# Products 5 and 7 in another order, and weights' lower parts by an adding DMA, in a two-block transformer layer kernel

## The chip, the cores and the metric

The kernel runs on one core of a Trainium2 chip. The metric is the device time of one execution, in microseconds. Engines are named as in the profile: PE (TensorE's matmuls) and PEld (its weight loads), DVE (VectorE), ACT (ScalarE), POOL (GpSimd) and SP (SyncE, which issues most DMAs here).

## What is computed

Two transformer blocks run one after the other on 512 tokens of width 1024; the first block puts 16 meta tokens in front (528 columns). Each block is a SwiGLU feed-forward layer, a token mixer, and another SwiGLU layer, with norms between them. All is in float32.

```python
def first_block(x, ...):                       # 16 + 512 tokens
    h = h + 0.5 * rmsnorm(swiglu(rmsnorm(h, gn[0]), ffn_w_in[0], ffn_w_out[0]), gn[1])
    y = mlstm_mixer(rmsnorm(h, gn[2]), a_w_in, a_conv_w, a_conv_b, a_gate_b, a_w_out)
    h = h + rmsnorm(y, gn[3])
    h = h + 0.5 * rmsnorm(swiglu(rmsnorm(h, gn[4]), ffn_w_in[1], ffn_w_out[1]), gn[5])
    return h[:, 16:]

def second_block(x, ...):                      # 512 tokens
    h = h + 0.5 * swiglu_2(rms_norm(h, ...), w_gate, w_up, w_down)
    proj = rms_norm(h, ...) @ w_in             # latent attention (8 heads) and retention (8 heads)
    h = h + concat([mla_group(...), retention_group(...)]) @ w_o
    h = h + 0.5 * swiglu_2(rms_norm(h, ...), w_gate, w_up, w_down)
    return rms_norm(h, final_norm)

def swiglu(x, w_in, w_out):                    # d_ff = 2816
    gu = x @ w_in
    return (silu(gu[..., :D_FF]) * gu[..., D_FF:]) @ w_out
```

## The kernel before, in words

**Split products.** Activations stand in SBUF with features on the partitions. Every large product is made of three matmuls in the round format fp32r: weights' higher part times activations' higher part, higher times lower, lower times higher. A weight tile of 128x1024 (a "unit") arrives by DMA in one of two raw tiles (`raw0`, `raw1`, and `rawx` beside them in the feed-forward layers). `Weights.pump` (from line 107) then splits it into a slot: ACT writes the rounded higher part `whi` (line 120), and `lo_engine` subtracts that from the raw tile and writes the lower part `wlo` (line 121). There are four to six slots; a unit is split as soon as a slot comes free, so some units stand ready ahead of PE. When the last unit of a raw tile is split, SP loads the next but one raw tile into it (`self.dma(r + 3)`).

`lo_engine` is DVE in the feed-forward layers and POOL in the two mixers: line 1129, from the fifth product of the first mixer (mLSTM), and line 1339, for the second mixer (latent attention and retention).

**Sevens.** In the feed-forward layers the last 16 of 22 chunks of 128 hidden features are computed by Strassen-Winograd products (`Ffn.seven`, from line 699; its matmuls are issued by `product`, line 696): seven products of 12 matmuls each in place of eight, over two halves of the tokens (264 or 256 columns). One chunk has P1 to P7. P1 and P2 use the unit "gates", P5 and P7 the unit "twos" (its first and second half), P6, P4 and P3 half units. P1, P6, P7 and P4 add up in one PSUM bank (`sa`, `o.a` in the code), with a copy to SBUF by ACT after P1, P6 and P7 (`m1`, `m2`, `m3`); P5 and P3 add up in another (`sc`, `o.c`), P2 has a third (`sb`). After P7 and P5, DVE makes `c22 = o.c + m3`. P4 and P3 of a chunk are written in the program inside the next chunk (`up_a(old)`, `gate_b(old)`). There are 8 runs of 8 chunks in the kernel: two in each of the four feed-forward layers.

A chunk's "gates" unit is split late: `W.hold` keeps it back until the copy `m3` of the chunk before, and `tc.issue_after(last.ins)` puts the cast behind that copy on ACT's queue.

**Order of the work.** The program is written as one sequence, and a scheduling layer then orders the instructions of each engine by its own estimate of when things are ready. So what stands in the source order (P5, P7, P1, P2, P4, P6, P3) is interleaved on PE's queue: parts of P4, P3, P1 and P2 stand mixed. Every engine works through its queue in order.

**Mixers.** In both mixers PE's queue alternates between the input projections (units of 24 matmuls, twice that over two column ranges in the first block) and attention steps. DVE and ACT evacuate, convolve, mask and normalize; POOL has some casts and subtractions of queries and keys (lines 1080, 1081, 1539), the masks (`affine_select`, line 1158), the lower parts of the weights (line 121) and a few DMAs.

Of the kernel before, what the change touches and what calls it, by code (L numbers as in the profile page):

```python
# [8 lines left out]
F32 = mybir.dt.float32  # L9
# [54 lines left out]
class Weights:  # L64
# [42 lines left out]
    def pump(self):  # L107
        nc = self.nc
        while self.n_split < len(self.subs):
            r, make, half = self.subs[self.n_split]  # L110
            if self.hold and self.raws[r][2] and self.raws[r][1] == 5:
                break
            idle = self.idle_halves if half else self.idle
            if not idle:
                break
            slot = idle.pop(0)
            self.dma(r + 1)
            unit, splits = make(self.raw_tiles[r], slot.hi, slot.lo)
            for ho, lw, src in splits:
                nc.scalar.copy(out=ho, in_=src)  # L120
                self.lo_engine.tensor_tensor(out=lw, in0=src, in1=ho.bitcast(F32), op=ALU.subtract)  # L121
            unit.slot = slot
            self.units.append(unit)
            self.n_split += 1
            self.raws[r][1] -= 1
            if self.raws[r][1] == 0:
                del self.raw_tiles[r]
            if self.raws[r][1] == 0:
                self.dma(r + 3)
            if self.raws[r][2] and self.raws[r][1] == 2 and self.n_raw == r + 2 and self.raws[r + 2][2]:  # L130
                self.load(r + 2, True)
# [88 lines left out]
def two_blocks(ctx: ExitStack, tc, d, out):  # L220
# [407 lines left out]
    class Ffn:  # L628
# [70 lines left out]
        def seven(self, fs, below):  # L699
# [25 lines left out]
            for f in fs:  # L725
                o = Unit(None, None)
                o.f = f
                (u,) = W.take(1)
                o.a, b = ps("sa")[:, 0:n], ps("sb")[:, 0:n]
                self.product(o.a, u, 0, "P1", True)  # L730
                m1 = yt("ht", n)
                act.copy(out=m1, in_=o.a)
                self.product(b, u, 1, "P2", True)
                o.s1, t = self.tmp("a", n), self.tmp("b", n)
                dve.tensor_tensor(out=o.s1, in0=b, in1=m1, op=ALU.add)
                act.activation(out=t, in_=o.s1, func=ACTF.Tanh, scale=0.5)
                W.release(u)
                if old:
                    up_a(old)
                dve.scalar_tensor_tensor(out=o.s1, in0=t, scalar=1.0, in1=o.s1, op0=ALU.add, op1=ALU.mult)  # L740
                (u,) = W.take(1)
                self.product(o.a, u, 0, "P6")
                o.m2 = yt("rp", n)
                act.copy(out=o.m2, in_=o.a)
                W.release(u)
                if old:
                    gate_b(old)
                (u,) = W.take(1)
                o.c = ps("sc")[:, 0:n]
                self.product(o.c, u, 0, "P5", True)  # L750
                self.product(o.a, u, 1, "P7")
                m3 = yt("sqFalse", n)
                last = act.copy(out=m3, in_=o.a)  # L753
                o.c22 = yt("sqacc", n)
                dve.tensor_tensor(out=o.c22, in0=o.c, in1=m3, op=ALU.add)
                W.hold = False
                with tc.issue_after(last.ins):
                    W.release(u)
                W.hold = True
                o.u2, o.u4 = W.take(2)  # L760
                old = o
# [364 lines left out]
    make = {"k": lambda n: item_qk("k", n), "q": lambda n: item_qk("q", n), "v": item_v, "o": item_o}  # L1126
    lead = [Item(1, ev_gate, done_gate)] + [make[k](n) for k, n in order[:3]]
    run_lead(lead, br)
    W.lo_engine = pool
    for k, n in order[3:6]:  # L1130
        run_item(make[k](n), AB)
    cm_s, sp = open_pool("mixs")
# [203 lines left out]
    close_pool(cm_w2)  # L1336


    W.lo_engine = pool
    cm_b, bp = open_pool("mixb")  # L1340
    hsp = drp.tile([P, KD, SEQ], F32, name="hsp")
    pool.dma_start(out=hsp, in_=h[:, :, NM:TT])
# [489 lines left out]
```

## Time and profile before

| | |
|---|---|
| median of 3 runs | 2091.21 us (2089.55 to 2098.18) |
| the profiled execution's own time | 2091.01 us |
| its span in the profile | 2089.1 us |
| PE busy | 2006.3 us, 96% of the span |
| PEld busy | 1840.6 us, 88% |
| DVE busy | 1549.0 us, 74% |
| ACT busy | 1027.4 us, 49% |
| POOL busy | 326.9 us, 16% |
| mean granted TensorE clock | 0.99 |

The time of a run lies 1.9 us above its span. PE's matmuls overlap: the next one starts before the last has drained, so start-to-start distances tell more than durations, and a stretch in which PE counts as busy may still run at the lower granted clock. The feed-forward layers fill about 0 to 400, 640 to 1400 and 1665 to 2060 us; the first mixer lies at about 400 to 640 us and the second at 1405 to 1665 us.

### The profile page before, as it was taken

To read this page: it belongs to the slowest core of one execution; us is meant where nothing else is said; L and a number is where in the kernel's file an instruction comes from. 1 tells how busy PE (TensorE), PEld (TensorE's weight loads), DVE (VectorE), ACT (ScalarE), POOL (GpSimd) and SP (SyncE) were. 2 spreads that over 40 slices of the span, in tenths; PEclk is the share of its full clock that TensorE was granted. 3 is DMA by queue.
4 is the path that set the end of the run, shared out by engine and by line. 5 is a ranking of instruction groups with operands and counts; after the bars stand their busy time and mean duration, and the time that the engine had idled before them with its cause. 6 is when DMAs were issued, how large, how long until landed. Compare 5 with 4: busy or idle time off the path is not lost.

```text
span 2089.1 us, 34858 instructions
## 1 busy us (share of the span) xinstructions
PE 2006.3 (96%) x13583; PEld 1840.6 (88%) x13583; DVE 1549.0 (74%) x2949; ACT 1027.4 (49%) x1973; POOL 326.9 (16%) x290
## 2 busy tenths in 40 slices
PE   8999999989999999999999999998999999999998
PEld 8999999988889989989998988987777778898998
DVE  6848477787886767758777775877888877676684
ACT  5445255445555445436443543654666643353462
POOL 0011020034430002011000201103222100010200
PEclk9999999999999999999999999999999999999999
DMA  6357565222223327567532766733112153475661
GB/s 186 96 111 152 147 140 135 72 77 81 87 81 110 79 79 156 145 137 146 162 80 77 154 152 137 148 118 104 47 47 61 41 141 100 107 158 133 147 151 55
DMA packets 387851, 237.01 MB, mean 113 GB/s; under 512 B 10427, under 2 KB 383926, under 8 KB 387686
## 3 DMA queue, kind: packets, MB, share of 16 engines
q1 hardware_dynamic: 317446, 192.94, 31.4%
q0 software_dynamic: 69680, 40.62, 14.1%
q8 instruction: 106, 1.74, 0.3%
q10 hardware_dynamic: 560, 1.24, 0.2%
q14 instruction: 59, 0.48, 0.1%
HBM read 230.53 MB, written 4.23 MB: 112 GB/s over the span
## 4 chain that ended last, share of the span: by engine, by line
PE 77%; DVE 12%; ACT 5%; issue 3%; POOL 1%; DMA 1%; ACTq 0%; POOLq 0%; DVEq 0%
PE dn L484 23%; PE sa L696 17%; PE acc L484 11%; PE sc L696 8%; PE sb L696 4%; PE accB L484 3%; PE accA L484 3%; PE wo L484 2%; DVE wlo L121 1%; DVE accF L1206 1%; ACT sqFalse L753 1%; PE p L419 1%; PE ro L1604 1%; ACT whi L120 1%; DVE cv L1067 1%
## 5 line engine op out<-in xcount | busy, mean ns | idle before, releaser
L120 ACT CAST whi<-raw 128x1024 fp32r<-128x1024 f32 (+3 forms) x500 | 392.8, 801 | 360.0 <-PE dn L484 163.2
L121 DVE TENSOR_TENSOR wlo<-raw,whi 128x512 fp32r<-128x512 f32 (+2 forms) x456 | 402.3, 905 | 112.9 <-ACT whi L120 110.4
L484 PE MATMUL dn<-gh,whi 128*128 128x256 f32 (+2 forms) x908 | 277.6, 326 | 0.5 <-ACT gh L465 0.5
L484 PE MATMUL dn<-gl,whi 128*128 128x256 f32 (+2 forms) x908 | 277.7, 326 | 0.0
L484 PE MATMUL dn<-gh,wlo 128*128 128x256 f32 (+2 forms) x908 | 276.9, 325 | 0.0
L484 PE MATMUL acc<-nh,whi 128*128 128x512 f32 (+2 forms) x600 | 196.4, 361 | 8.9 <-DVE y L1212 3.9
L484 PE MATMUL acc<-nl,whi 128*128 128x512 f32 (+2 forms) x600 | 192.0, 355 | 0.0
L484 PE MATMUL acc<-nh,wlo 128*128 128x512 f32 (+2 forms) x600 | 191.6, 354 | 0.0
L484 PEld LDWEIGHTS dn<-gh,whi 128*128 128x128 f32 x908 | 163.0, 188 | 16.5 <-ACT gh L465 0.7
L484 PEld LDWEIGHTS dn<-gh,wlo 128*128 128x128 f32 x908 | 163.1, 188 | 15.0
L484 PEld LDWEIGHTS dn<-gl,whi 128*128 128x128 f32 x908 | 163.0, 188 | 15.1
L696 PE MATMUL sa<-nh,whi 128*128 128x256 f32 (+1 forms) x488 | 142.5, 292 | 24.9 <-ACT sqFalse L753 24.9
L696 PE MATMUL sc<-nh,wlo 128*128 128x256 f32 (+1 forms) x488 | 137.4, 282 | 0.0
L696 PE MATMUL sa<-nh,wlo 128*128 128x256 f32 (+1 forms) x488 | 137.3, 281 | 0.0
L696 PE MATMUL sc<-nh,whi 128*128 128x256 f32 (+1 forms) x488 | 137.2, 281 | 0.0
L696 PE MATMUL sa<-nl,whi 128*128 128x256 f32 (+1 forms) x488 | 137.1, 281 | 0.0
L696 PE MATMUL sc<-nl,whi 128*128 128x256 f32 (+1 forms) x488 | 137.0, 281 | 0.0
L484 PEld LDWEIGHTS acc<-nh,whi 128*128 128x128 f32 (+1 forms) x600 | 108.1, 194 | 25.9 <-DVE z L1054 4.5
L696 PEld LDWEIGHTS sa<-nh,whi 128*128 128x128 f32 x488 | 91.8, 188 | 34.9 <-ACT sqFalse L753 34.7
L484 PEld LDWEIGHTS acc<-nh,wlo 128*128 128x128 f32 (+1 forms) x600 | 107.0, 194 | 15.5
L484 PEld LDWEIGHTS acc<-nl,whi 128*128 128x128 f32 (+1 forms) x600 | 106.8, 193 | 13.9
L95 POOL DMA_DIRECT2D raw<-in_ffn_w_up x32 | 41.1, 1285 | 455.9 <-DMA raw<-in_ffn_w_up 245.4
(492 smaller groups left out, 5569.5 us busy)
## 6 DMA issues: line engine op xcount, KB each, us to landing
raw<-in_ffn_w_in SPq DMA_DIRECT2D x56, 512.0 KB, 3.9
raw<-in_ffn_w_gate SPq DMA_DIRECT2D x44, 512.0 KB, 3.7
raw<-in_ffn_w_in SPq DMA_DIRECT2D x64, 256.0 KB, 3.2
raw<-in_ffn_w_out SPq DMA_DIRECT2D x16, 1024.0 KB, 7.7
raw<-in_ffn_w_up SPq DMA_DIRECT2D x64, 256.0 KB, 3.3
raw<-in_ffn_w_down SPq DMA_DIRECT2D x16, 1024.0 KB, 7.2
raw<-in_a_w_in SPq DMA_DIRECT2D x18, 512.0 KB, 3.6
rawx<-in_ffn_w_in SPq DMA_DIRECT2D x32, 256.0 KB
```

Source lines behind the costliest of these rows:

```text
L95: self.nc.gpsimd.dma_start(out=dst(t), in_=src, accum_op=ALU.add)
L120: nc.scalar.copy(out=ho, in_=src)
L121: self.lo_engine.tensor_tensor(out=lw, in0=src, in1=ho.bitcast(F32), op=ALU.subtract)
L419: pe.matmul(self.p1[:, self.n:self.n + 2], lhsT=src[:, o:o + P], rhs=ones[:, 0:2], start=True, stop=True)
L484: pe.matmul(p, lhsT=w[:, k], rhs=cut(x, k, sl), start=(k == 0 and j == 0), stop=(k == last and j == 2))
L696: pe.matmul(acc, lhsT=w[:, 4 * i + k], rhs=x[:, k], start=start and k == 0 and j == 0, stop=k == 3 and j == 2, skip_group_check=not start)
L753: last = act.copy(out=m3, in_=o.a)
L1067: dve.scalar_tensor_tensor(out=v, in0=z[:, t0 + j:t0 + j + n], scalar=col(V_CW + 8 * j + c), in1=v, op0=ALU.mult, op1=ALU.add)
L1206: dve.reciprocal(out=dn, in_=dn)
L1604: pe.matmul(o[i], lhsT=vt_[:, i, j], rhs=s_[i, j][b], start=(j == 0 and b == 0), stop=(j == 3 and b == 1))
```

## The change

In a chunk of sevens that has a chunk before it, P7 (which goes into the bank that P4 also needs, and which ACT copies) is issued ahead of P5. In both mixers the lower part of a weight is now made in two steps: ACT writes the rounded negative of the raw tile into `wlo`, and a DMA issued by POOL adds the raw tile to it in place. POOL's subtraction is gone there. The first chunk of each run keeps its order, and the feed-forward layers keep DVE for the lower parts.

```diff
             for ho, lw, src in splits:
                 nc.scalar.copy(out=ho, in_=src)
-                self.lo_engine.tensor_tensor(out=lw, in0=src, in1=ho.bitcast(F32), op=ALU.subtract)
+                if self.lo_engine is None:
+                    nc.scalar.activation(out=lw, in_=src, func=ACTF.Copy, scale=-1.0)
+                    nc.gpsimd.dma_start(out=lw.bitcast(F32), in_=src, accum_op=ALU.add)
+                else:
+                    self.lo_engine.tensor_tensor(out=lw, in0=src, in1=ho.bitcast(F32), op=ALU.subtract)
...
                 (u,) = W.take(1)
                 o.c = ps("sc")[:, 0:n]
-                self.product(o.c, u, 0, "P5", True)
+                if not old:
+                    self.product(o.c, u, 0, "P5", True)
                 self.product(o.a, u, 1, "P7")
                 m3 = yt("sqFalse", n)
                 last = act.copy(out=m3, in_=o.a)
+                if old:
+                    self.product(o.c, u, 0, "P5", True)
                 o.c22 = yt("sqacc", n)
                 dve.tensor_tensor(out=o.c22, in0=o.c, in1=m3, op=ALU.add)
...
     run_lead(lead, br)
-    W.lo_engine = pool
+    W.lo_engine = None
...
-    W.lo_engine = pool
+    W.lo_engine = None
     cm_b, bp = open_pool("mixb")
```

The change moves instructions on the engines' queues. First, PE's queue at the end of the second chunk of the first run of sevens. `sc_1684` and `sa_1597` are that chunk's two banks, `sa_1728` and `sb_1729` those of the next chunk; P5 and P7 read the weights `whi1_108`, P4 reads `whi0_114`, P1 and P2 the gates in `whi2_110`. Before:

```order
L696 MATMUL sc_1684<-nh_81,whi1_108 128x264
...
L696 MATMUL sa_1597<-nh_81,whi1_108 128x264
...
L696 MATMUL sa_1597<-nh_81,wlo1_109 128x264
L696 MATMUL sa_1597<-nh_81,whi0_114 128x264
...
L696 MATMUL sa_1728<-xh0_733,whi2_110 128x264
L696 MATMUL sa_1728<-xl0_734,whi2_110 128x264
L696 MATMUL sb_1729<-xh1_735,whi2_110 128x264
L696 MATMUL sb_1729<-xl1_736,whi2_110 128x264
L696 MATMUL sa_1597<-nh_81,wlo0_115 128x264
```

With the change (the matmul of `product` is now at line 700):

```order
L700 MATMUL sa_1597<-nh_81,whi1_108 128x264
...
L700 MATMUL sc_1684<-nh_81,whi1_108 128x264
...
L700 MATMUL sc_1684<-nh_81,wlo1_109 128x264
L700 MATMUL sa_1728<-xh0_733,whi2_110 128x264
L700 MATMUL sa_1728<-xl0_734,whi2_110 128x264
L700 MATMUL sb_1729<-xh1_735,whi2_110 128x264
L700 MATMUL sb_1729<-xl1_736,whi2_110 128x264
L700 MATMUL sa_1597<-nh_81,whi0_114 128x264
```

Before, eight matmuls of P4 stand directly behind P7, in P7's own bank, and four of the next chunk's P1 and P2 after them. Now P7's twelve stand ahead, P5's twelve behind them, and directly behind P5 four matmuls of P1 and P2, which need the gates of the next chunk; P4 follows.

Second, ACT's queue at the end of the third chunk (`sqFalse` is the copy `m3`; `whi1_108` at full width, 1024, is the next chunk's gates). Before:

```order
L753 COPY sqFalse_1840<-sa_1728 128x264
L120 CAST whi1_108<-raw1_86 128x1024
L120 CAST whi2_110<-raw1_86 128x512
L120 CAST whi2_110<-rawx1_732 128x512
L120 CAST whi0_114<-raw1_86 128x512
```

With the change:

```order
L758 COPY sqFalse_1828<-sa_1728 128x264
L120 CAST whi1_108<-raw1_86 128x1024
L469 CAST gh_97<-sqFalse_1807 128x264
L120 CAST whi2_110<-raw1_86 128x512
L120 CAST whi2_110<-rawx1_732 128x512
```

The cast of the gates stays directly behind the copy `m3`, which now waits for P7 alone, 12 matmuls earlier in the chunk.

Third, POOL's queue in the first mixer, at one head (`Abc` and `accF` are rows broadcast for a head, `w` its mask). Before:

```order
L1147 DMA accF<-AEd 128x512
L121 TENSOR_TENSOR wlowide<-raw_85,whiwide 128x1024
L1158 AFFINE_SELECT w<-Abc 128x128 x2
L1158 AFFINE_SELECT w<-Abc 128x16
L1142 DMA Abc<-AEd 128x512
L1081 TENSOR_TENSOR k_5692<-cv,k_5692 64x528
L121 TENSOR_TENSOR wlo_111<-raw_86,whi_110 128x1024
```

With the change:

```order
L1154 DMA accF<-AEd 128x512
L123 DMA wlowide<-raw_85 128x1024
L1165 AFFINE_SELECT w<-Abc 128x128 x2
L1165 AFFINE_SELECT w<-Abc 128x16
L1149 DMA Abc<-AEd 128x512
L1088 TENSOR_TENSOR k_5699<-cv,k_5699 64x528
L123 DMA wlo_111<-raw_86 128x1024
```

A DMA stands where each subtraction stood, and the rest keeps its order. On ACT's queue there is one more instruction for each, the negative copy at line 122, mostly directly behind the cast of the higher part and at places up to five instructions later. POOL has 57 of them in all: 41 of 128x1024 (21 in the first mixer), and 16 smaller ones for the four units that `add_mla` (line 356) makes in the second mixer (pieces of 384, 64, 64 and 256 columns).

## Rows read from the trace of the kernel before

**Rows 1.** The profile page, parts 1 and 4: busy time of each engine with its share of the span and instructions, and the chain that ended last by engine.

```profile
PE 2006.3 (96%) x13583; PEld 1840.6 (88%) x13583; DVE 1549.0 (74%) x2949; ACT 1027.4 (49%) x1973; POOL 326.9 (16%) x290
PE 77%; DVE 12%; ACT 5%; issue 3%; POOL 1%; DMA 1%; ACTq 0%; POOLq 0%; DVEq 0%
```

**Rows 2.** The waits of PE over the whole span: who waited for whom; us in total, times, longest.

```profile
PE sa L696 <- ACT sqFalse L753: 24.9, 48, 0.5
PE p L451 <- DVE dg L450: 9.2, 9, 3.9
PE rs L1589 <- DVE rk L1536: 7.8, 3, 3.0
PE aT L1035 <- DVE y L1024: 6.9, 1, 6.9
PE acc L484 <- DVE y L1212: 3.9, 2, 2.0
PE acc L484 <- DVE z L1054: 3.7, 3, 1.2
```

**Rows 3.** PE's timeline at the boundary between two chunks of sevens: start, duration, engine, line, instruction. The first row is the last matmul of P7, the next two the first two of P4, and the last row the first one of the next chunk's P1, seven starts behind the third.

```profile
155.28 0.28 PE L696 MATMUL sa<-nh,wlo 128*128 128x264 f32 x1
156.09 0.39 PE L696 MATMUL sa<-nh,whi 128*128 128x264 f32 x1 [0.52 <-ACT sqFalse L753]
156.31 0.28 PE L696 MATMUL sa<-nl,whi 128*128 128x264 f32 x1
...
157.18 0.29 PE L696 MATMUL sa<-xh,whi 128*128 128x264 f32 x1
```

**Rows 4.** The timelines of ACT and DVE at the same boundary: the copy `m3`, the cast of the next chunk's gates, and the lower part of those gates (with a second subtraction of half the width, 1.83 us for both).

```profile
155.66 0.38 ACT L753 COPY sqFalse<-sa 128x264 f32<-128x264 f32 x1 [0.54 <-PE sa L696]
155.93 1.05 ACT L120 CAST whi<-raw 128x1024 fp32r<-128x1024 f32 x1
157.01 1.83 DVE L121 TENSOR_TENSOR wlo<-raw,whi 128x1024 fp32r<-128x1024 f32 x2 [0.52 <-ACT whi L120]
```

**Rows 5.** POOL's groups of instructions over the span: line, engine, operation, names, shapes, count, busy us, mean ns of one, idle time before.

```profile
L121 POOL TENSOR_TENSOR wlo<-raw,whi 128x1024 fp32r<-128x1024 f32 x32 | 77.4, 2419 | 166.6 <-ACT whi L120 144.8 <-PE rs L1590 11.8 <-PE mkv L1430 9.5
...
L95 POOL DMA_DIRECT2D raw<-in_ffn_w_up x32 | 41.1, 1285 | 455.9 <-DMA raw<-in_ffn_w_up 245.4 <-DVE raw L311 133.6 <-DVE b L651 39.0
...
L121 POOL TENSOR_TENSOR wlowide<-raw,whiwide 128x1024 fp32r<-128x1024 f32 x9 | 21.7, 2414 | 36.8 <-ACT whiwide L120 36.7
...
L1142 POOL DMA_DIRECT2D Abc<-AEd x8 | 4.5, 563 | 4.9 <-ACT w L1162 2.6 <-POOL w L1158 1.5 <-PE den L1198 0.8
```

**Rows 6.** Timelines of POOL and DVE in the first mixer: two of POOL's subtractions, and DVE instructions beside them and away from them.

```profile
504.40 2.40 POOL L121 TENSOR_TENSOR wlowide<-raw,whiwide 128x1024 fp32r<-128x1024 f32 x1 [0.77 <-ACT whiwide L120]
505.07 2.29 DVE L1067 SCALAR_TENSOR_TENSOR cv<-z,vec,cv 128x528 f32<-128x528 f32 x1 [1.01 <-ACT cv L1064]
508.69 1.55 DVE L1067 SCALAR_TENSOR_TENSOR cv<-z,vec,cv 128x528 f32<-128x528 f32 x2
522.13 0.61 DVE L466 TENSOR_TENSOR sl<-w,sh 128x432 fp32r<-128x432 f32 x1
535.25 2.38 POOL L121 TENSOR_TENSOR wlo<-raw,whi 128x1024 fp32r<-128x1024 f32 x1
535.39 2.68 DVE L466 TENSOR_TENSOR sl<-w,sh 128x400 fp32r<-128x400 f32 x1 [0.32 <-ACT sh L465]
```

**Rows 7.** Stretches of the two mixers: length, then busy us (and instructions) of PE, PEld, DVE, ACT and POOL, the granted clock, the DMA engines' share, GB/s.

```profile
444.00:456.00 12.00, 5.07 (x39) 4.78 (x38) 11.75 (x14) 3.89 (x7) 4.02 (x3) 0.85 0.15 44
...
520.00:530.00 10.00, 8.02 (x48) 7.34 (x47) 8.81 (x14) 5.73 (x13) 4.31 (x6) 0.83 0.22 59
...
1430.00:1446.00 16.00, 11.42 (x41) 9.01 (x40) 13.03 (x24) 8.56 (x15) 5.20 (x2) 0.79 0.20 54
...
436.00:640.00 204.00, 185.64 (x1174) 168.96 (x1173) 170.98 (x190) 99.28 (x192) 91.63 (x99) 0.95 0.29 85
1405.00:1660.00 255.00, 237.08 (x1183) 190.66 (x1182) 214.97 (x430) 162.99 (x322) 65.52 (x49) 0.98 0.20 57
```

**Rows 8.** DVE's timeline in the second mixer: the start of the square-root iteration behind a norm, and the last sum ahead of the retention keys.

```profile
1431.26 2.27 DVE L380 TENSOR_SCALAR nw_y<-nw_v 128x4 int32<-128x4 int32 x1
...
1548.36 2.47 DVE L1529 TENSOR_TENSOR t<-t 128x512 f32<-128x512 f32 x1
```

**Rows 9.** One group of ACT in the second mixer (columns as in rows 5), and DMA issues of the whole span: queue, count, KB each, median us from issue to landing.

```profile
L120 ACT CAST whi<-raw 128x1024 fp32r<-128x1024 f32 x16 | 16.8, 1051 | 17.9 <-issue 6.7 <-PE acc L484 5.1 <-PE dn L484 3.1
...
raw<-in_a_w_in SPq DMA_DIRECT2D x18, 512.0 KB, 3.6
rawx<-in_ffn_w_gate POOLq DMA_DIRECT2D x32, 256.0 KB, 6.7
raw<-in_ffn_w_up POOLq DMA_DIRECT2D x32, 256.0 KB, 5.3
hsp<-h POOLq DMA_DIRECT2D x1, 2048.0 KB, 9.9
```

**Rows 10.** Timelines: the subtraction for a unit of the first mixer and the first matmul that reads that unit; then a DMA issue on POOL in the sevens and the DVE subtraction beside it.

```profile
445.02 2.40 POOL L121 TENSOR_TENSOR wlowide<-raw,whiwide 128x1024 fp32r<-128x1024 f32 x1 [3.29 <-ACT whiwide L120]
...
491.67 0.51 PE L484 MATMUL acc<-nh,whiwide 128*128 128x272 f32 x2
...
163.03 1.28 POOL L95 DMA_DIRECT2D raw<-in_ffn_w_in  x1 [8.63 <-DVE raw L311]
163.22 0.69 DVE L121 TENSOR_TENSOR wlo<-raw,whi 128x512 fp32r<-128x512 f32 x1
```

## The prediction

> **What bounds the kernel now.** I read the page first: PE is busy 96% of the span and holds 77% of the chain that ended last, DVE 12% [rows 1]. So a change can pay only where PE stands still or runs slowly, and PE's list of waits says where that is [rows 2]. Its longest line by far is the one that the reordering aims at: 48 waits in the sevens, 24.9 us, for ACT's copy `m3`. Nearly all that follow are waits for DVE, and they lie in the two mixers. There the stretches are the view to read [rows 7]: from 436 to 640 us PE is idle for 18.4 us and the granted clock is 0.95, from 1405 to 1660 us it is idle for 17.9 us at 0.98. Around an idle stretch the clock falls to its lower level (0.85, 0.83 and 0.79 in the pieces shown), so idle time is paid for a second time. Five per cent of 204 us and two of 255 us are 10 and 5 us. In all, 36 us idle and some 15 us of clock are what the second part can give back at the very most.
>
> **Part 1, P7 ahead of P5.** Now P4 stands right behind P7 in P7's own bank and must wait until ACT has copied it. From the last matmul of P7 to the second of P4 are 1.03 us (155.28 to 156.31) [rows 3]. Undisturbed, matmuls start every 0.124 us (seven starts from 156.31 to 157.18), so two starts would take 0.25 us. **A boundary loses 0.78 us**, more than the 0.52 us of the wait shown, since the pipeline drains and fills again. 48 boundaries lose 37.6 us.
>
> With the change the 12 matmuls of P5 cover the copy: 12 x 0.124 = 1.49 us against 0.76 us from 155.28 to the copy's end at 156.04. That wait goes. What is late next: the new queue has four matmuls of the next chunk's P1 and P2 right behind P5, and their gates are cast by ACT only after `m3`. The cast begins 0.65 us after P7's last start and takes 1.05 us, so it ends at 156.98 [rows 4]. In the present queue eight matmuls of P4 lie ahead of P1, which starts at 157.18, and the cast is just hidden. In the new queue P1's weight load would come at 155.28 + 1.49 = 156.77, but gets its weights at 157.03 (the 0.05 us from the copy's end to the matmul at 156.09 added). It is 0.26 us late, and a restart costs 0.10 us more (0.22 us in place of 0.124 between the two starts behind the wait). **A new wait of about 0.36 us takes the place of one of 0.78 us**, a gain of 0.42 us at 48 boundaries: 20 us. In 36 of them the halves are 256 columns, P5 is a little shorter and the lateness a little larger, so I take 19 us. The bounds are 37.6 us, if the cast comes in time, and nothing. The gates' lower part hides: DVE needs about 1 us behind the cast and ends near 158.0, the first matmul that reads it comes ten matmuls behind 157.03, after 158.2. DVE's sum `c22` has to wait for P5 now, but P5 ends where P7 ended, and its first reader, P3, comes some 50 matmuls later. The copy `m2` must now be done when P3 alone has passed (1.49 us, before P3's rest and P5): a copy of that size takes 0.38 us [rows 4].
>
> **Part 2, the lower parts in the mixers.** Removed are 41 subtractions of 128x1024, 2.42 us each, and 16 small ones on POOL [rows 5]. POOL itself is no bound (91.6 of 204 us busy, 65.5 of 255 us [rows 7]); what they cost shows on DVE. While the subtraction at 504.40 runs, a DVE instruction that takes 0.78 us elsewhere takes 2.29 us and ends as it ends; beside the one at 535.25 a subtraction of 0.6 us takes 2.68 us [rows 6]. In the second mixer the first step of the iteration behind a norm, on 4 columns, takes 2.27 us, and ahead of the retention keys a sum of two 128x512 tiles, a size that takes 0.69 us in [rows 10], takes 2.47 us [rows 8]. So each subtraction holds DVE for 1.5 to 2.1 us when it meets such an instruction.
>
> How much of that PE gets back goes by its waits. First mixer: the wait for `aT` (6.9 us) hangs on a DVE stretch that is busy throughout (11.75 of 12 us [rows 7]); two subtractions lie in its way, some 4.4 us. The waits at the heads (3.9 and 3.7 us in five places, and smaller ones) are 1.2 to 2.0 us each, about one held instruction; they should go almost wholly, with the clock that they cost. From 18.4 us of idle time I take 11 us, and 7 of the 10 us of clock: **18 us**. Second mixer: 4 us ahead of a norm's broadcast (its longest wait is 3.9 us, two held instructions stand before it), with 3 us of clock (16 us at 0.79 [rows 7]), and 4 of the 7.8 us in front of the retention scores, since there ACT is the next in line: 11 us, less 1 us for small waits of PE for ACT that grow. **10 us**.
>
> Added: 57 negative copies on ACT. No row shows that form; the cast of the same size takes 1.05 us [rows 9], and I take that; the bounds are nothing, where ACT waits anyway, and 41 x 1.05 = 43 us if all stood on the path. ACT has the room: 99 of 204 us busy, 163 of 255 us. Their price on the path is within the shares that I took. Added on POOL: 57 DMA issues at 0.56 us (128 rows) to 1.29 us (512 pieces) [rows 5], less than the 2.42 us which they replace, except that pieces of 512 bytes from two-unit raw tiles may take twice 1.29 us. POOL's masks behind them come no later than now. An issue doesn't hold DVE: beside the one at 163.03 a DVE subtraction takes its usual 0.69 us [rows 10].
>
> The lower part arrives later. No row has an addition of 512 KB inside SBUF: 256 KB added from DRAM land after 5.3 to 6.7 us, a plain 2048 KB after 9.9 us [rows 9]. I take 8 us, between 5.3 and twice 6.7 us. It hides: the unit made at 445.02 is first read at 491.67 [rows 10]. The raw tile is held longer too. Two raw tiles serve 21 units in 204 us, 9.7 us each, so a tile may take 19.4 us: 2.1 us on ACT, about 1 us on POOL, 8 us, and 3.6 us for the next load are 14.7 us. Loads are so far not late, and PE has no wait for a weight in its list. The Trainium skill (DMA: Bandwidth & Descriptors, Anatomy of one DMA) gives 2.0 us plus the bytes over 436 GB/s for a DMA that POOL issues. By it 256 KB would land after 2.6 us, where the rows show 5.3 to 6.7 us, and 512 KB after an estimated 3.2 us; the sum would be the same, and the slower rival below would lose its chance.
>
> **The sum.** 19 + 18 + 10 = 47 us off the profiled execution's own time of 2091.0 us (1.9 us above its span and 0.2 us below the median): **2044 us**.
>
> **The rivals.** *Gates too late* (chance 0.15): the cast of the gates, or their lower part, comes later than reckoned, and the new wait eats the old one. For it speaks that P1's lead of eight matmuls is gone; the margin of the lower part is a few tenths. Then part 1 gives 3 us: 2060 us. *Gates in time* (0.15): the scheduler's four matmuls meet a finished cast; part 1 gives 37 us: 2026 us. *ACT in DVE's place* (0.16): the second copy delays the exponentials and casts that DVE and PE wait for, and the mixers give 8 us: 2064 us. For it: ACT's 163 of 255 us in the second mixer, on short chains; against it: the first mixer, half idle. This takes in the case that an issue on POOL holds DVE after all. *Raw tiles too late* (0.05, slower than before): landing plus the rest exceeds 19.4 us per tile. That begins at a landing of 12.7 us, just under twice 6.7 us. At 18 us a unit takes 12.4 us, 2.7 us too much for 41 units, 110 us; slots filled ahead take back about 30 us, part 1 another 19 us, and the mixers' gain is void: 2150 us. It turns slower from about 16 us on. The forecast has 0.49.
>
> **Range and chances.** Most of what is uncertain is how much of 51 us the mixers return and whether the gates' cast is hidden. The low end, 2021 us, is near the case with the gates in time and the mixers as forecast; the high end, 2069 us, takes in both cases where one part fails. A difference under about 0.5% (10.5 us) is not told from none here. Faster by more than that: 0.90; the same: 0.05, where both parts fail together; slower: 0.05.
>
> **What would show it.** Right: the 48 waits for the copy `m3` are gone from PE's list, with a smaller one for the cast of the gates, or only a gap of 0.3 us between starts, in their place; in the mixers no DVE sum or subtraction takes over 2 us, except beside POOL's query and key work; the wait for `aT` is under 3 us, and the clock in the heads is 1.00. POOL's DMA for a unit lands within 6 to 11 us, and PE waits for no lower part. Wrong: PE waits for `whi` or `wlo` in the mixers; ACT's casts come later than now, with PE waiting for ACT; or chunks of the sevens that still take 11.0 us.

## The result and the profile after

The changed kernel took **2036.4 us** (median of 4 runs, 2033.0 to 2037.0) against 2094.1 us (2089.6 to 2098.2) for the kernel before on the same chip: ratio 0.972, 95% interval 0.9695 to 0.9748. Faster, as forecast (2044 us, range 2021 to 2069); the forecast was 7.6 us too slow. Between the two profiled executions the gain is 54.0 us (2091.0 to 2037.0), and the shares below are shares of that.

The profiled execution took 2037.0 us, with a span of 2035.2 us. Parts 1 and 4 of its page answer to [rows 1]:

```profile
PE 1995.0 (98%) x13583; PEld 1833.5 (90%) x13583; DVE 1486.4 (73%) x2949; ACT 1063.4 (52%) x2030; POOL 283.2 (14%) x290
PE 84%; DVE 8%; ACT 4%; DMA 2%; issue 1%; POOL 0%; ACTq 0%; POOLq 0%; DVEq 0%; SPq 0%
```

Of the chain that ended last, DVE has lost four points, and PE has gained seven. PE's waits, from the longer ones, answer to [rows 2]:

```profile
PE p L455 <- DVE dg L454: 6.0, 7, 1.8
...
PE mo L1504 <- DVE pl L470: 5.1, 4, 1.6
PE ro L1611 <- ACT rsh L469: 2.3, 3, 1.1
PE sa L700 <- ACT ht L736: 2.0, 4, 1.1
```

The 48 waits for the copy `m3` are gone, and so are those for `aT` (6.9 us) and for the retention keys `rk` (7.8 us). Three have come up, or grown, that were not forecast by name: `pl` and `rsh` in the second mixer, and ACT's copy `m1` (`ht`) in the sevens.

**Where the time came from.** For every kernel here the span is cut at the eight runs of sevens (from the start of the first matmul of `product` in a run to the start of the last one). The stretch between the second run and the third holds the first mixer, with the feed-forward parts next to it, that between the sixth and the seventh the second mixer; the rest is start, end and the other stretches between runs. Microseconds, from one profile of each:

| kernel | eight runs of sevens | first mixer | second mixer | rest | span |
|---|---|---|---|---|---|
| before | 710.0 | 434.4 | 446.6 | 498.1 | 2089.1 |
| after | 689.2 | 412.4 | 434.1 | 499.5 | 2035.2 |
| sevens_only | 689.7 | 435.3 | 445.8 | 498.7 | 2069.5 |
| mixers_only | 710.2 | 410.8 | 435.3 | 498.0 | 2054.3 |
| gates_in_halves | 685.6 | 410.6 | 433.7 | 499.9 | 2029.8 |
| gates_early | 683.6 | 408.9 | 438.3 | 499.5 | 2030.3 |
| gates_early_2 | 671.6 | 410.7 | 433.9 | 498.2 | 2014.4 |
| lo_by_dve | 689.0 | 415.4 | 441.1 | 498.5 | 2044.0 |
| pool_reads_too | 690.7 | 408.4 | 450.5 | 498.1 | 2047.7 |
| act_copy_twice | 690.4 | 417.9 | 435.2 | 499.0 | 2042.5 |
| old_order_gates_early | 671.9 | 411.5 | 435.0 | 499.4 | 2017.8 |

So after against before: 20.8 us out of the sevens, 22.0 out of the first mixer, 12.5 out of the second, 1.4 us more in the rest. The first mixer's stretch reads 408 to 412 us in seven kernels that do the same there: differences of 4 us in that column say nothing. The piece between the second run of sevens and the mixer itself shows where this scatter comes from: the same work took 86.1 us at a granted clock of 0.98 before, 88.2 us at 0.96 after, and 84.1 us at 1.00 in pool_reads_too.

**The boundary of the sevens.** PE's timeline, the place that answers to [rows 3]: the last matmul of P5, then the first three of the scheduler's four of the next chunk's P1 and P2 (P4 comes behind those).

```profile
156.03 0.28 PE L700 MATMUL sc<-nh,wlo 128*128 128x264 f32 x1
156.34 0.39 PE L700 MATMUL sa<-xh,whi 128*128 128x264 f32 x1
156.57 0.28 PE L700 MATMUL sa<-xl,whi 128*128 128x264 f32 x1
156.69 0.28 PE L700 MATMUL sb<-xh,whi 128*128 128x264 f32 x1
```

And ACT's, with DVE's subtraction behind it, answering to [rows 4]:

```profile
154.96 0.38 ACT L758 COPY sqFalse<-sa 128x264 f32<-128x264 f32 x1 [0.50 <-PE sa L700]
155.24 1.05 ACT L120 CAST whi<-raw 128x1024 fp32r<-128x1024 f32 x1
...
156.32 1.23 DVE L125 TENSOR_TENSOR wlo<-raw,whi 128x1024 fp32r<-128x1024 f32 x1 [0.93 <-ACT whi L120]
```

The copy `m3` ends at 155.34, while P5's last matmul starts at 156.03. Then P1's first matmul starts 0.31 us after P5's last in place of 0.124, just behind the end of the gates' cast at 156.29, and the next 0.23 us after it. **A boundary loses 0.30 us**; a whole chunk of 264 columns takes 10.53 us from start to start in place of 11.04. PE's list of waits has no line for it, since its matmuls drain for most of the gap. The list of the weight loads (PEld), which come ahead of the matmuls, has all 48, with the gates' cast as what ended the wait (us in total, times, longest):

```profile
PEld sa L700 <- ACT whi L120: 10.6, 44, 0.2
...
PEld sa L700 <- ACT whiwide L120: 1.0, 4, 0.2
```

**The mixers.** The stretches that answer to the first and to the last two of [rows 7], cut at the same places in PE's queue by the count of its matmuls (columns as there):

```profile
442.80:447.40 4.60, 4.60 (x40) 4.38 (x38) 4.53 (x8) 0.70 (x1) 0.00 (x0) 1.00 0.42 114
...
434.80:614.70 179.90, 176.88 (x1174) 162.71 (x1173) 137.81 (x190) 118.30 (x213) 66.41 (x99) 0.99 0.72 154
1368.50:1612.00 243.50, 231.79 (x1183) 187.04 (x1182) 196.23 (x433) 185.69 (x360) 47.09 (x49) 1.00 0.52 108
```

The 39 matmuls that took 12 us, at a clock of 0.85, now take 4.6 us without a gap, at 1.00. The work of the first mixer takes 179.9 us in place of 204: PE's idle time fell from 18.4 to 3.0 us, and the clock rose from 0.95 to 0.99. That of the second takes 243.5 us in place of 255: idle time fell from 17.9 to 11.7 us, and the clock rose from 0.98 to 1.00. In the first ACT has 19 us more to do and DVE 33 us less, in the second ACT 23 us more and DVE 19 us less. Why DVE has less, two of its groups show, in the first mixer, first in the kernel before (count, busy us, mean ns, idle before):

```profile
L466 DVE TENSOR_TENSOR sl<-w,sh 128x400 fp32r<-128x400 f32 x8 | 12.7, 1590 | 5.9 <-ACT sh L465 5.9
L1120 DVE SCALAR_TENSOR_TENSOR y<-oth,y 128x512 f32<-128x512 f32 x5 | 10.7, 2143 | 0.8 <-ACT oth L1119 0.8
```

and then in the changed one (the last group over the whole span, where it has the same five):

```profile
L470 DVE TENSOR_TENSOR sl<-w,sh 128x400 fp32r<-128x400 f32 x8 | 4.6, 574 | 9.9 <-ACT sh L469 9.8
L1127 DVE SCALAR_TENSOR_TENSOR y<-oth,y 128x512 f32<-128x512 f32 x5 | 3.5, 692 | 3.4 <-ACT oth L1126 3.4
```

The same instructions take 0.57 and 0.69 us in place of 1.59 and 2.14. A count over all of DVE's instructions between the sevens says the same. In the kernel before 24 in the first mixer and 16 in the second take over 0.3 us more than the shortest of their form, 37.8 and 22.0 us in all, and every one lies beside arithmetic of POOL. In the changed kernel 6 and 2 are left, 3.8 and 0.8 us, all beside POOL's query and key work. The two that [rows 8] showed (2.27 and 2.47 us) take 0.17 and 0.68 us:

```profile
1407.39 0.17 DVE L384 TENSOR_SCALAR nw_y<-nw_v 128x4 int32<-128x4 int32 x1
...
1547.22 0.68 DVE L1536 TENSOR_TENSOR t<-t 128x512 f32<-128x512 f32 x1
```

What was added: ACT's negative copies, POOL's DMA issues, and the landing of the addition (the last row: KB each, median us).

```profile
L122 ACT ACTIVATE wlo<-raw 128x1024 fp32r<-128x1024 f32 x32 | 33.9, 1058 | 0.1
L123 POOL DMA_DIRECT2D wlo<-raw x44 | 49.9, 1308 | 213.4 <-ACT wlo L122 169.4 <-ACT rv L469 20.6 <-PE p L455 9.0
wlo<-raw POOLq DMA_DIRECT2D x32, 512.0 KB, 5.3
```

### The profile page after: what moved, and what is told of

It reads as the page before. It is cut to its first block, busy times and chain, and to the rows that moved or that the text cites. A ratio compares the mean times of both kernels' runs of the same rounds, so it can differ in the third digit from the quotient of the medians.

```text
span 2035.2 us, 34893 instructions
## 1 busy us (share of the span) xinstructions
PE 1995.0 (98%) x13583; PEld 1833.5 (90%) x13583; DVE 1486.4 (73%) x2949; ACT 1063.4 (52%) x2030; POOL 283.2 (14%) x290
## 4 chain that ended last, share of the span: by engine, by line
PE 84%; DVE 8%; ACT 4%; DMA 2%; issue 1%; POOL 0%; ACTq 0%; POOLq 0%; DVEq 0%; SPq 0%
PE dn L488 25%; PE sa L700 18%; PE acc L488 14%; PE sc L700 8%; PE sb L700 4%; PE accB L488 3%; PE accA L488 3%; PE wo L488 2%; DVE wlo L125 1%; ACT whi L120 1%; PE ro L1611 1%; PE p L423 1%; PE num L1202 1%; PE ms L1469 1%; DMA raw<-in_w_uq 1%
## 5 line engine op out<-in xcount | busy, mean ns | idle before, releaser
L120 ACT CAST whi<-raw 128x1024 fp32r<-128x1024 f32 (+3 forms) x500 | 397.5, 801 | 346.3 <-PE dn L488 168.5
L488 PE MATMUL acc<-nh,whi 128*128 128x512 f32 (+2 forms) x600 | 191.0, 353 | 1.1 <-DVE y L1219 1.1
L700 PE MATMUL sa<-nh,whi 128*128 128x256 f32 (+1 forms) x488 | 137.3, 281 | 0.0
L488 PEld LDWEIGHTS acc<-nh,whi 128*128 128x128 f32 (+1 forms) x600 | 104.6, 188 | 16.4 <-DVE y L1219 1.6
L95 POOL DMA_DIRECT2D raw<-in_ffn_w_in x32 | 41.1, 1283 | 439.4 <-DMA raw<-in_ffn_w_in 163.6
```

Of the source, the lines that this page charges most:

```text
L95: self.nc.gpsimd.dma_start(out=dst(t), in_=src, accum_op=ALU.add)
L488: pe.matmul(p, lhsT=w[:, k], rhs=cut(x, k, sl), start=(k == 0 and j == 0), stop=(k == last and j == 2))
L700: pe.matmul(acc, lhsT=w[:, 4 * i + k], rhs=x[:, k], start=start and k == 0 and j == 0, stop=k == 3 and j == 2, skip_group_check=not start)
```

## The experiments

All ratios are to the kernel before, run beside the kernel named, each with its 95% interval. Each edit is one to the changed kernel, unless the text names another.

**Each part alone: sevens_only.** `lo_engine` stays POOL in both mixers.

```diff
-    W.lo_engine = None
+    W.lo_engine = pool
```

> The reordering alone: P7 ahead of P5, the mixers' subtractions on POOL as before. Theory (the two parts add up, and a boundary of the sevens loses 0.30 us in place of 0.78): the eight runs of the sevens take 20 to 21 us less together, every other stretch is as before, so 0.990 of the time before (some 2073 us by the profiled executions). Rival one (gates in time): 37 us less, ratio 0.982. Rival two (gates too late, and the gain seen with both parts together came out of the adding DMA, which frees POOL and DVE): 3 us less, ratio 0.998. The stretch with the first mixer stays at 434 us and the one with the second at 447 us under each of them; if they shrink, the mixers' gain is not the DMA's.

Measured: 2071.9 us, ratio 0.9907 (0.9889 to 0.9925). The sevens' runs take 20.3 us less than before, the mixers 0.9 us more and 0.8 less. The waits that the second part removed are all there:

```profile
PE p L455 <- DVE dg L454: 9.0, 7, 3.9
PE rs L1596 <- DVE rk L1543: 7.8, 3, 3.0
PE aT L1042 <- DVE y L1031: 6.9, 1, 6.9
```

Both rivals on the gates fall: 37 us and 3 us were their prices.

**mixers_only.** P5 is issued ahead of P7 in every chunk.

```diff
-                if not old:
-                    self.product(o.c, u, 0, "P5", True)
+                self.product(o.c, u, 0, "P5", True)
                 self.product(o.a, u, 1, "P7")
...
-                if old:
-                    self.product(o.c, u, 0, "P5", True)
```

> The adding DMA alone: P5 ahead of P7 as before. Theory: the first mixer's stretch falls by 22 us (434 to 412), the second's by 12 (447 to 434), the runs of the sevens stay as before with their 48 waits for the copy m3 (91.5, 89.3, 89.0 us and so on): 34 us less, ratio 0.9837. Rival (the parts help each other, for instance since POOL's queue is freer for the sevens' own adding DMAs): the runs of the sevens shrink here too, or the mixers give under 25 us.

Measured: 2055.4 us, ratio 0.9827 (0.9812 to 0.9843). The first mixer gives 23.6 us, the second 11.3, the sevens nothing (710.2 against 710.0), and their old wait is back:

```profile
PE sa L700 <- ACT sqFalse L757: 24.9, 48, 0.5
```

The parts add up: 20.3 and 34.9 us alone, 55.3 us in the three columns together.

**What a boundary still loses: gates_in_halves.** The gates' cast and subtraction in two pieces of 128x512.

```diff
-            return cut_of(hi, lo, 2), [(hi[:, 0:1024], lo[:, 0:1024], t[0][:, 0:1024])]
+            return cut_of(hi, lo, 2), [(hi[:, c:c + 512], lo[:, c:c + 512], t[0][:, c:c + 512]) for c in (0, 512)]
```

> Both parts, and the cast of the gates (128x1024, 1.05 us on ACT) in two pieces of 128x512 (0.62 us each), with DVE's subtraction in two pieces as well. Theory: what a boundary still loses (0.30 us: 0.19 ahead of P1's first matmul and 0.11 behind it) is the wait for the gates' cast, which now ends 0.43 us sooner for P1, ahead of P5's end; that wait goes. But P1's third matmul now reads the lower part, and DVE's first piece (0.68 us behind the first cast) ends about 0.2 us too late for it. So a boundary loses 0.1 to 0.3 us, and the runs of the sevens take 0 to 10 us less than with both parts alone: 2027 to 2036 us, ratio to the kernel before 0.968 to 0.973. Rival (the remaining 0.30 us is not the cast's but a cost of changing the bank): nothing moves, and the gap of 0.3 us stays ahead of P1's first matmul.

Measured: 2032.2 us, ratio 0.9719 (0.9702 to 0.9735); the sevens take 3.6 us less than after. PE's timeline at the same boundary, from P5's last matmul:

```profile
156.02 0.29 PE L700 MATMUL sc<-nh,wlo 128*128 128x264 f32 x1
156.14 0.28 PE L700 MATMUL sa<-xh,whi 128*128 128x264 f32 x1
156.26 0.28 PE L700 MATMUL sa<-xl,whi 128*128 128x264 f32 x1
156.62 0.39 PE L700 MATMUL sa<-xh,wlo 128*128 128x264 f32 x1
```

The gap ahead of P1 has gone (0.12 us from P5's last start), so it was the cast, not the change of bank. And it has come back two matmuls later, ahead of the first that reads the lower part, as expected. The weight loads' list has moved with it, from ACT's cast to DVE's subtraction (a second line has the other 4 boundaries):

```profile
PEld sa L700 <- DVE wlo L125: 9.6, 44, 0.3
```

What both cost together is the question of the next two runs.

**gates_early.** On top of that, both pieces of the cast stand on ACT behind the tanh of the chunk before and ahead of the copy `m3`. While `W.only` is set, `pump` splits the gates and nothing else.

```diff
+                o.tanh = act.activation(out=t, in_=g, func=ACTF.Tanh, scale=0.5)
+                if early:
+                    W.hold, W.only = False, True
+                    with tc.issue_after(o.tanh.ins):
+                        W.pump()
+                    W.hold, W.only = True, False
...
+                    with tc.issue_after(W.cast.ins):
+                        last = act.copy(out=m3, in_=o.a)
```

> Both parts, the gates' cast in two pieces, and both pieces placed on ACT ahead of the copy m3, behind the tanh of the chunk before, where ACT stands idle for 0.5 us. Theory: the casts end before P5 does, the first lower part about 0.9 us before P1's third matmul, and the copy m3, now some 0.7 us later, still ends before P4 needs its bank, since P1 and P2 stand ahead of P4 now. A boundary loses nothing: 0.30 us x 48 = 14 us less than with both parts alone, 2022 us, ratio to the kernel before 0.9665. Rival one: the gates' raw tile lands too late for the earlier place, ACT waits for the DMA, and the copy m3 and all behind it come later: runs of the sevens as long as with both parts alone or longer, with waits of PE for ACT or of ACT for the raw tile. Rival two (bank change): the gap of 0.3 us stays.

Measured: 2034.8 us, ratio 0.9729 (0.9712 to 0.9746): no gain in the time, though the sevens take 5.6 us less in the profiled execution, the fastest of the four. The forecast of 2022 us failed. In the first two runs of sevens six chunks each take 10.22 us from start to start, against 10.53 after; in later runs single chunks take up to 11.2 us. One of these places, on ACT and then on PE:

```profile
812.31 0.62 ACT L125 CAST whi<-raw 128x512 fp32r<-128x512 f32 x1 [2.64 <-PE sa L707]
812.83 0.36 ACT L749 COPY ht<-sa 128x256 f32<-128x256 f32 x1
```

```profile
812.03 0.28 PE L707 MATMUL sa<-nh,wlo 128*128 128x256 f32 x1
813.25 0.39 PE L707 MATMUL sa<-whiwide,whi 128*128 128x256 f32 x1 [0.94 <-ACT ht L749]
```

The cast of the twos, no longer tied to the copy `m3`, was ordered ahead of the copy `m1` (`ht`); it waits 2.64 us for its slot, and `m1` and PE wait behind it. It was not the raw tile that came late, as the first rival had it, but the order of the casts behind the gates.

**gates_early_2.** The other casts are held back until `m3` again: `W.rest` is set from the gates' early cast to the release behind `m3`.

```diff
-            if self.only and not gates:
+            if self.only and not gates or self.rest:
                 break
```

> As gates_early, but the casts behind the gates' (three, twos, ups of the next chunk) keep their old place behind the copy m3. In gates_early six boundaries of the first two runs took 10.22 us in place of 10.53, and in later runs single chunks lost 0.3 to 1.5 us, where a cast of the twos stood on ACT ahead of the copy m1 and waited 2.6 us for its slot. Theory: with that order mended every boundary gives its 0.30 us: the runs of the sevens take 14 us less than with both parts alone (675 against 689 us), 2022 us, ratio to the kernel before 0.967. Rival: the raw tile of the gates lands too late in the later runs, chunks of 10.2 us stay irregular, and the gain is 6 us or less.

Measured: **2016.6 us**, ratio 0.9641 (0.9628 to 0.9654), the fastest kernel here, 17 us below the changed one by the two ratios and 20 by the medians. The chunks take 10.22 us at 264 columns and 9.91 to 10.00 us at 256 (after: 10.53 and 10.21 to 10.31), in all eight runs, and the sevens 17.6 us less than after: 48 x 0.30 = 14.4 us, and most of the rest from four waits for `m1` that the change had brought (below). The boundary on ACT, and PE from P5's last matmul on:

```profile
152.66 0.42 ACT L729 ACTIVATE b<-sqFalse 128x264 f32<-128x264 f32 x1 [1.62 <-DVE sqFalse L728]
152.99 1.13 ACT L125 CAST whi<-raw 128x512 fp32r<-128x512 f32 x2
154.05 0.41 ACT L476 CAST gh<-sqFalse 128x264 fp32r<-128x264 f32 x1
154.37 0.37 ACT L774 COPY sqFalse<-sa 128x264 f32<-128x264 f32 x1
```

```profile
154.72 0.29 PE L707 MATMUL sc<-nh,wlo 128*128 128x264 f32 x1
154.84 0.28 PE L707 MATMUL sa<-xh,whi 128*128 128x264 f32 x1
...
155.09 0.28 PE L707 MATMUL sa<-xh,wlo 128*128 128x264 f32 x1
```

No start is over 0.13 us behind the one before, the left-out one at 154.97 among them, and the weight loads' list has no line for `sa` any more. The copy `m3` now ends at 154.74, and nothing waits for it, since P4 stands 24 matmuls behind P5.

**Is the reordering needed then? old_order_gates_early.** As gates_early_2, with P5 ahead of P7 again (the edit of mixers_only).

> As gates_early_2 (gates cast in two pieces ahead of the copy m3, the other casts behind it), but with P5 ahead of P7 again, as in the kernel before. Now the scheduler puts the next chunk's P1 and P2 behind P7, and P4, which needs the bank that m3 empties, comes 24 matmuls (2.9 us) later. Theory (a boundary loses only what stands behind P7 in its own bank before ACT is through with it, whatever the product is that covers it): the copy is covered without the reordering too, a boundary loses nothing, and the time is that of gates_early_2 within 0.2%, 2013 to 2021 us, ratio to the kernel before 0.964. Rival (P7 last costs by itself, since m3 and DVE's sum c22 come 1.5 us later): the waits for m3 or for the sum come back and the runs of the sevens take 14 to 35 us more, 2031 to 2052 us.

Measured: 2019.3 us, ratio 0.9650 (0.9636 to 0.9663), the sevens 671.9 us against 671.6. So once the gates come early the first part of the change is worth 0.3 us in the sevens, and no more than some 3 us in the whole time (the medians differ by 2.7 us, the intervals of the ratios overlap): the scheduler then puts P1 and P2 of the next chunk between P7 and P4, and they cover the copy as P5 does. What cost 0.78 us at a boundary was P4 right behind P7, and P4 stood there because the gates, and with them P1, came late.

**What the second part saved: lo_by_dve.** DVE makes the lower parts in the mixers.

```diff
-    W.lo_engine = None
+    W.lo_engine = dve
```

> Both parts, but in the mixers DVE makes the weights' lower parts (1.23 us for 128x1024) in place of ACT's negative copy and the DMA; POOL has none of it. Theory (what POOL's subtraction cost was DVE's time: 28.6 us of held instructions in the first mixer, some 19 in the second, and DVE's is what PE waits for): DVE pays 21 x 1.23 = 26 us and 20 x 1.23 = 25 us itself, so the mixers give little of their 34 us: stretches of 425 to 435 and 437 to 447 us, 2050 to 2070 us in all. Rival (the gain came from the lower part being late off a slow POOL, or from POOL's queue): with a faster maker and an empty POOL the stretches stay at 412 and 434 us or fall further, 2036 us or less.

Measured: 2044.7 us, ratio 0.9779 (0.9765 to 0.9794): below the range expected, by the first mixer (the second is inside it). The stretches are 415.4 and 441.1 us, so DVE's own subtractions leave 19.0 of the first mixer's 22.0 us and 5.5 of the second's 12.5. Yet DVE is nearly as busy as in the kernel before, or busier: 162.4 and 220.9 us on the same matmuls, against 171.0 and 215.0 us in [rows 7] and 137.8 and 196.2 us in the changed kernel:

```profile
433.40:616.80 183.40, 177.84 (x1174) 163.57 (x1173) 162.35 (x211) 99.55 (x192) 44.96 (x78) 0.98 0.32 94
1370.00:1619.70 249.70, 233.15 (x1183) 188.62 (x1183) 220.87 (x471) 164.73 (x325) 9.44 (x13) 0.99 0.21 61
```

So some 25 us more of DVE's time in each mixer lengthen these stretches by 3.5 and 6.2 us. My theory, that DVE's time is what counts, falls in this form. What this run leaves is two readings: that it matters which instruction the time falls on, or that POOL's lower parts were late. Against the second speaks that in the kernel before neither the matmuls nor the weight loads of the two mixers have a wait for a lower part that POOL makes.

**pool_reads_too.** In the second mixer POOL does its subtraction as well, into a scratch tile that nobody reads.

```diff
                     nc.gpsimd.dma_start(out=lw.bitcast(F32), in_=src, accum_op=ALU.add)
+                    if self.scratch is not None and len(src.shape) == 3 and src.shape[1] * src.shape[2] == 1024:
+                        nc.gpsimd.tensor_tensor(out=grid(self.scratch, src.shape[1]), in0=src, in1=ho.bitcast(F32), op=ALU.subtract)
```

> Both parts, and in the second mixer alone POOL does its old subtraction as well, behind the issue of the adding DMA, from the same raw tile and upper part into a scratch tile that nobody reads (128x1024, 16-bit result). No consumer waits for it; only POOL's reading and time are back. Theory (POOL's two-input pass holds DVE): DVE instructions of over 2 us are back in the second mixer, and its stretch goes from 434 us back to 443 to 447 us; the first mixer's stays at 412 us. 2046 us, ratio 0.977. Rival (the gain is that the lower part left POOL's chain of waits, or that the DMA is the faster maker): the stretch stays within 2 us of 434 us.

Measured: 2048.5 us, ratio 0.9795 (0.9782 to 0.9809). The second mixer's stretch is 450.5 us, 16.4 more than after and above the 443 to 447 us expected, and the first mixer has kept its gain. One place, on POOL and on DVE:

```profile
1377.68 2.73 POOL L126 TENSOR_TENSOR scratch<-raw,whi 128x1024 bf16<-128x1024 f32 x1
```

```profile
1377.33 3.11 DVE L391 TENSOR_TENSOR nw_u<-nw_g,nw_y 128x4 f32<-128x4 f32 x1
1380.48 0.16 DVE L392 SCALAR_TENSOR_TENSOR nw_y<-nw_u,nw_y 128x4 f32<-128x4 f32 x1
```

A step on 4 columns that takes 0.16 us elsewhere takes 3.11 us, and ends 0.03 us after POOL's subtraction. PE's waits for what hangs on such steps are back:

```profile
PE p L458 <- DVE dg L457: 8.3, 8, 3.8
PE rs L1600 <- DVE rk L1547: 5.6, 3, 2.0
```

By the count above, 14 instructions of DVE are stretched in the second mixer here, by 21.2 us in all, as against 22.0 us in the kernel before. No lower part comes from POOL's subtraction here, and no matmul waits for one, so in the second mixer it is the held instruction, not the late lower part. The price is 4 us above what the kernel before paid there; the copies and the DMA issues, which are still there too, may be why, but no run shows it. For the first mixer this was not tried. There the counts and groups above speak for the same, with the missing waits for lower parts; that is an argument from traces, not an experiment.

**act_copy_twice.** The negative copy is written twice.

```diff
                     nc.scalar.activation(out=lw, in_=src, func=ACTF.Copy, scale=-1.0)
+                    nc.scalar.activation(out=lw, in_=src, func=ACTF.Copy, scale=-1.0)
```

> Both parts, with ACT's negative copy done twice over (the same copy, written again, ahead of the DMA): 41 x 1.06 = 43 us and a few us of small ones more on ACT in the mixers. Theory (ACT's copies are hidden, since ACT has room and its order on the short chains is not the bound): the mixers' stretches grow by 2 to 8 us together. Rival (the copy already stands in DVE's place on the path, and what the mixers gave is net of it): 17 us or more, as much as a second copy on the path would take.

Measured: 2039.6 us, ratio 0.9754 (0.9739 to 0.9769), 7 us above after by the two ratios and 3 by the medians. By the stretches it is 5.5 us more in the first mixer, not far outside the scatter there, and 1.1 in the second. 43 us of added work on ACT cost some 7 at most: ACT is covered, and "ACT in DVE's place" falls.

## Why the prediction was right, step by step

The sum was 47 us; the three columns of the table give 55.3, and the rest takes 1.4 back. The three places and the three mechanisms were those forecast, and each gave somewhat more than its term.

**Part 1: 19 us forecast, 20.8 measured** (20.3 alone). The boundary lost 0.78 us before and loses 0.30 now, where 0.36 was forecast, at the place and for the reason given: P1 waits for the gates' cast, as the weight loads' list says. The cast started 0.28 us after the start of `m3`, as before, and took the 1.05 us of [rows 4]; the runs with the cast in halves and early show that it was the cause. 48 x 0.48 = 23 us. Some 2.6 us of them were lost to a wait that the prediction did not have, so that its number came out near by two misses of opposite sign: in the last chunk of four runs, two casts of the next stage are ordered ahead of the copy `m1`, and PE waits up to 1.1 us for it. Rows of ACT and PE in the changed kernel:

```profile
202.27 1.56 ACT L120 CAST whi<-raw 128x1024 fp32r<-128x1024 f32 x2 [2.01 <-PE sb L700]
203.74 0.37 ACT L736 COPY ht<-sa 128x264 f32<-128x264 f32 x1
...
204.16 0.39 PE L700 MATMUL sa<-whiwide,whi 128*128 128x264 f32 x1 [1.06 <-ACT ht L736]
```

It is in sevens_only too (2.8 us, 4 times) and not in mixers_only, so it comes with the reordering. About 1 us more at the start of the program does not: up to the first run of sevens it is 126.9 us before and 128.1 after, but 127.1 in gates_early_2, which has the reordering, and 128.3 in old_order_gates_early, which has not. Its cause is open.

**Part 2, first mixer: 18 us forecast, 22.0 measured.** The mechanism is the one forecast, POOL's subtraction holding DVE instructions. Its two sizes were low: 11 of 18.4 us of idle time were counted, and 15.3 came back; of the clock's 10 us 7 were counted, and the 24.1 us saved between the same matmuls leave nearly 9 for it. The table's 22.0 us is less, since the piece ahead of the mixer took 2.1 us longer at the lower clock of 0.96. The wait for `aT` was to fall by 4.4 us to under 3 and is gone. One reading of [rows 6] was loose: the held instructions do not end as POOL's does, but 0.56 and 0.44 us behind it, most of their own time (0.78 and 0.6 us). They look as if they had stood still until POOL was through and then run.

**Second mixer: 10 us forecast, 12.5 measured.** Idle time gave 6.2 us (8 forecast), and 5.3 of the 11.5 us saved between the same matmuls are left for the clock (3 forecast, from one piece of it). The small waits for ACT that were to take 1 us back are `rsh` and `ph` (2.3 and 1.1 us). The 5.1 us for DVE's `pl`, which mixers_only has as well, are the next thing late there.

**Added work.** The negative copy takes 1.06 us (1.05 taken) and is covered. The DMA issue takes 1.31 us in the mean of the largest group, just above what was given, and 0.85 to 2.56 us in single ones. The landing was mis-sized: 5.3 us in the median for 512 KB (one took 11.6), where 8 was taken and 6 to 11 stated as the test, so that sentence was wrong, to the good side. By the prediction's own sum the raw tile is then held for some 12 us in place of 14.7, with 19.4 to spend, and PE's list has no wait for a lower part in the mixers. By the figures of the Trainium skill (DMA: Bandwidth & Descriptors, Anatomy of one DMA) the estimate was 3.2 us; the measurement lies between that and mine, and decides.

**The rivals.** Gates too late (2060 us) and gates in time (2026 us): between them, as forecast. What the second asks for at a boundary is what gates_early_2 shows, where 0.30 us more came back at each. ACT in DVE's place: not seen (act_copy_twice). POOL's issues do not hold DVE: beside the DMA issues alone the DVE instructions of both mixers keep their usual times, within 0.1 us. Raw tiles too late: not seen.

**What I had wrong beyond the sum** is why the held instructions cost what they do. Before lo_by_dve I took DVE's lost time for the price. DVE can spend the same time on subtractions of its own, which its queue places where it has room, for 10 us of the 34 (3.0, which is within the scatter, and 7.0). About the same time, stretched over whichever instruction happens to meet POOL's subtraction, cost 34, since some of these instructions stand in front of PE. The Trainium skill (SBUF — State Buffer, Who interferes with whom) has a rule for it: VectorE's second pair of SBUF ports is GpSimd's only one; a VectorE instruction with two SBUF inputs contends with a GpSimd one that reads SBUF, and the shared pair is an exclusive lock. The held step of 3.11 us, which has two SBUF inputs and ends 0.03 us after POOL's, agrees; the records put its start 0.35 us ahead of POOL's, so they do not settle which of the two came first. The step of 2.27 us in [rows 8] has one SBUF input; the rule as given here does not speak of it.

## What to carry to other kernels

Before reordering around a wait, ask why the waiting work stands there: here one late cast set both the place of P4 and what the reorder left over, and moving that cast made the reorder all but needless. Read the list of the weight loads beside that of the matmuls: a wait too short for the second stood in the first, 48 times. When one cast is moved forward, tie down those behind it, or the scheduler moves them too. Work on POOL that reads two SBUF tiles beside a DVE with short chains is priced by the DVE instructions it may hold, and a spare engine with a DMA can take it over even if it does more work in all.

## What the runs showed of the hardware

- An addition of 512 KB from SBUF to SBUF by a DMA that POOL issues landed in 5.3 us (median of 32), about when 256 KB added from DRAM do (5.2 and 6.8 us in the same run).
- With these DMAs the DMA engines' share rose from 0.29 to 0.72 in the first mixer (85 to 154 GB/s), and no wait of PE for its weights appeared there.
- POOL's subtraction takes 2.4 us with a 16-bit result that nobody reads as it did with the 32-bit one (a median of 2405 ns against the mean of 2419 in [rows 5]), and holds DVE alike: it is not the result's width that does it.
